# Token rows stored before their norm and scaled after the fetch, token numbers worked out first, and empty rows left out of the fetch

## The chip, the cores and the metric

The kernel runs on one core of a Trainium2 chip. The metric is the device time of one execution in microseconds (us); lower is better. Engines are named as in the profile: PE (matrix), DVE (vector), ACT (scalar), POOL (GpSimd) and SP, which here only issues transfers. Sixteen DMA engines of the core carry the transfers out.

## What is computed

Two decoder layers over 512 tokens of width 1024. Each has a mixer, a cross-attention into 256 memory tokens and a mixture of 32 experts; after each of the three a residual sum is normalised. Only the last part matters here:

```python
def layer_norm(x, g, b, eps=LN_EPS):
    return _standardize(x, eps) * g + b
...
    g_prob = jax.nn.softmax(g_logits, axis=-1)
    grp = jnp.argmax(g_logits, axis=-1)
    ...
    top_v, top_i = lax.top_k(e_logits, MOE_TOPK)
    gate = (jax.nn.softmax(top_v, axis=-1) * p_grp).astype(x.dtype)
    expert = (grp[:, None] * MOE_PER_GROUP + top_i).astype(jnp.int32)
...
        h = jax.nn.silu(xb @ w_gate[e]) * (xb @ w_up[e])
        return h @ w_down[e]
...
        h = layer_norm(DN_ALPHA * h + xa, ln2_g[layer], ln2_b[layer])
        ff = hier_moe(h, ...)
        h = layer_norm(DN_ALPHA * h + ff, ln3_g[layer], ln3_b[layer])
```

A token goes to one of four groups of experts and to two of the eight experts there, so a layer has 1024 pairs of token and expert. An expert has a hidden width of 512; its three weight matrices are 2 MB each in float32.

## The kernel before

**Tiles.** The 512 tokens are four row tiles of 128 (`NT` is 4, `P` is 128). `h` holds them all in SBUF. An expert has 64 slots for tokens, and two experts share the 128 partitions: the lower 64 are one expert's slots, the upper 64 the other's. So there are 16 pairs, objects `X[0]` to `X[15]` of `ExpertRows` (L1660). Slots are filled from number 0 upwards; tokens that find no slot would go through `overflow` (L1757), whose loop runs no time on this input.

**Ahead of the experts.** The output projection of the cross-attention makes row tile after row tile of `h`; after each, `Router.step(i)` (L635) runs: it transposes the tile before (`turn`, PE and two `L612` copies on ACT), works out its router logits, normalises it in place (`norm`, L614, which shares the 1024 columns between DVE, ACT and POOL) and stores it to a DRAM array `rows` by ACT's queue (`store`, L618 and L619). Row 0 of `rows` is zero; token t is row t+1. The logits come from the un-normed transpose, and mean and scale are put in afterwards (L628, L629). `finish` (L647) does the last row tile; its norm lies on ACT (L172) and POOL (L173, L174). The mean and scale of a tile come from a chain of tiny DVE instructions (`ln_3...`, L132 to L160; the figure is the row tile).

**Routing** (L1543 to L1657) is mostly small DVE work: maxima, first-hit masks, ranks, and from these for each token and expert a slot. Then for each of the two choices a one-hot of the slot (L1643, 128x512, tile `hhs`) is multiplied on PE (L1649) with the token's number and gate, which gives a table by slot and pair: `ptab`. Its numbers become `idx` (L1655), its gates `tab`. Both choices' one-hots use one tile.

**A pair.** `gather` (L1680) fetches 128 rows of `rows` by an indirect transfer of POOL's queue into `xg`; an empty slot has number 0 and fetches the zero row. `turn` (L1686) transposes it on PE (`px`, L1693) and DVE copies it to `xT` (two copies, 128x512). `first` multiplies with the gate and up weights (`pg`, `pu`, L1704), L1708 to L1719 make silu(g)*u and transpose it, `second` (L1721) multiplies with the down weights (`py`, L1730) and scales by the gate into `wy` (ACT L1736, then DVE L1737). `combine` (L1740s) adds a pair's rows to `h` by a one-hot product (`pc`) one pair later. `moe` (L1844) writes PE's order of these out by hand; the other engines' is the scheduler's. The fetch for pair n+2 is issued after the transposes of pair n+1, since `xg` is one buffer; pair 15's is issued late, behind `overflow`, and its product closes the layer. `accumulate` (L631, L633) scales `h` for the residual sum once the rows are stored.

**Weights.** A ring of 20 tiles of 1 MB is loaded by SP's queue (L104) in the order of use, 12 loads a pair, each as soon as its tile is free. It fills while routing still runs, and goes on when the first `pg` has read its weights.

## Time and profile before

| | us |
|---|---|
| three timed runs | 1999.49, 1994.82, 1999.64 |
| their median | 1999.49 |
| the profiled execution | 1995.74 |
| its span on the core | 1994.0 |
| PE busy / DVE / ACT / POOL | 1794.0 / 958.7 / 448.9 / 273.9 |
| first pairs apart (layer 0) | 27.45 |
| later pairs apart | 31.09 |

The experts of layer 0 take the span from about 570 to 1030 us, those of layer 1 from about 1497 to 1950. In the rows below a time line has its start, its length, the engine, the line of the code, the operation, what it writes and reads, the shapes, and in brackets how long the engine was idle before and what ended that.

### The profile page before, as it was taken

What the parts mean: (1) busy time and instruction counts of PE and PEld (TensorE: products, weight loads), DVE (VectorE), ACT (ScalarE), POOL (GpSimd) and SP (SyncE); (2) the same over time, 40 slices, a digit from 0 to 9 for tenths busy, and PEclk for the clock granted to TensorE, in tenths of its full rate; (3) what the DMA queues carried; (4) which work ended last, traced back from release to release, by engine and by line L of the source; (5) the groups of instructions that cost most, each with busy time, mean ns of one, the idle gap of its engine ahead of it and who ended that gap; (6) DMA issues with size and microseconds to landing.
All of it is one profiled execution on the core that took longest, in us unless ns stands there. A gap on an engine that the chain in (4) does not pass through costs nothing. (4 is left out here: it accounts for less than half of the span.)

```text
span 1994.0 us, 23447 instructions
## 1 busy us (share of the span) xinstructions
PE 1794.0 (90%) x9206; PEld 1106.6 (55%) x9206; DVE 958.7 (48%) x2053; ACT 448.9 (23%) x834; POOL 273.9 (14%) x226
## 2 busy tenths in 40 slices
PE   8778998999969999989896999989969999989885
PEld 5567876878824334434346866778853334434332
DVE  5686456855633333323326566484572233323325
ACT  6313322343210000000022555443320000000000
POOL 3532433310110000000022100130020000000002
PEclk9887989999979999999998999999979999999998
DMA  5210105464779999999995200243678999999993
GB/s 186 64 63 26 50 1 201 157 201 146 298 302 419 420 420 420 421 421 420 422 373 171 85 22 22 88 143 124 264 283 357 420 420 421 420 420 420 421 420 126
DMA packets 124338, 522.41 MB, mean 262 GB/s; under 512 B 11936, under 2 KB 45888, under 8 KB 75584
## 3 DMA queue, kind: packets, MB, share of 16 engines
q1 hardware_dynamic: 114576, 486.58, 61.7%
q0 software_dynamic: 7056, 25.89, 3.7%
q10 hardware_dynamic: 2592, 8.40, 1.0%
q8 instruction: 74, 1.21, 0.2%
q14 instruction: 40, 0.33, 0.0%
HBM read 506.14 MB, written 14.69 MB: 261 GB/s over the span
## 5 line engine op out<-in xcount | busy, mean ns | idle before, releaser
L1704 PE MATMUL pu<-wu,xT 128*64 128x512 f32 x1024 | 241.9, 595 | 27.7 <-DMA wu<-in_moe_w_up_dram 27.7
L1704 PE MATMUL pg<-wg,xT 128*64 128x512 f32 x1024 | 235.3, 599 | 1.1 <-issue 0.8
L1710 DVE TENSOR_TENSOR hh<-hh,pu 128x512 f32<-128x512 f32 x32 | 22.0, 687 | 444.7 <-PE pu L1704 444.7
L1730 PE MATMUL py<-wd,hh 128*64 128x512 f32 x1024 | 228.9, 596 | 1.6 <-DVE hh L1719 1.6
L1736 ACT ACTIVATE wy<-py,tab 128x512 fp32r<-128x512 f32 x64 | 43.7, 687 | 635.6 <-PE py L1730 635.6
L1704 PEld LDWEIGHTS pu<-wu,xT 128*64 128x64 f32 x1024 | 78.3, 137 | 182.4 <-issue 127.0
L1744 PE MATMUL pc<-wy,wc 128*128 128x512 f32 x480 | 139.2, 420 | 27.8 <-DVE h L1754 27.8
L1704 PEld LDWEIGHTS pg<-wg,xT 128*64 128x64 f32 x1024 | 81.6, 138 | 145.1 <-issue 132.5
L1754 DVE TENSOR_TENSOR h<-h,pc 128x512 f32<-128x512 f32 x240 | 151.0, 680 | 8.6 <-PE pc L1744 8.6
L1683 POOL DMA_INDIRECT xg<-rows,idx x32 | 30.2, 945 | 859.3 <-PE px L1693 716.3
L1730 PEld LDWEIGHTS py<-wd,hh 128*64 128x64 f32 x1024 | 71.1, 137 | 135.5 <-issue 128.8
L1744 PEld LDWEIGHTS pc<-wy,wc 128*128 128x128 f32 x480 | 81.5, 189 | 86.1 <-DVE h L1754 50.4
L1737 DVE SCALAR_TENSOR_TENSOR wy<-py,tab,wy 128x512 fp32r<-128x512 f32 x64 | 47.8, 750 | 169.3 <-ACT wy L1736 165.7
L219 DVE TENSOR_TENSOR wl<-wt,wh 128x1024 fp32r<-128x1024 f32 x37 | 48.0, 1304 | 58.3 <-ACT wh L218 57.9
L218 ACT CAST wh<-wt 128x1024 fp32r<-128x1024 f32 x50 | 51.7, 1049 | 107.5 <-PE ptm L214 61.8
L212 PE MATMUL ptm<-wh,oh 128*128 128x512 f32 x192 | 75.7, 394 | 0.0
L214 PE MATMUL ptm<-wh,ol 128*128 128x512 f32 x192 | 75.0, 391 | 0.0
L213 PE MATMUL ptm<-wl,oh 128*128 128x512 f32 x192 | 75.0, 391 | 0.0
L1708 ACT ACTIVATE hh<-pg 128x512 f32<-128x512 f32 x32 | 19.1, 597 | 229.5 <-PE pg L1704 229.5
L212 PE MATMUL pcm<-xh,wh 128*128 128x512 f32 x144 | 61.9, 430 | 7.1 <-ACT xh L218 6.9
L214 PE MATMUL pcm<-xh,wl 128*128 128x512 f32 x144 | 60.9, 423 | 0.5 <-DVE wl L219 0.5
L213 PE MATMUL pcm<-xl,wh 128*128 128x512 f32 x144 | 60.6, 421 | 0.1
(532 smaller groups left out, 3358.1 us busy)
## 6 DMA issues: line engine op xcount, KB each, us to landing
wg<-in_moe_w_gate_dram SPq DMA_DIRECT2D x128, 1024.0 KB, 19.8
wu<-in_moe_w_up_dram SPq DMA_DIRECT2D x128, 1024.0 KB, 21.1
wd<-in_moe_w_down_dram SPq DMA_DIRECT2D x124, 1024.0 KB, 20.1
wr<-in_ab_w_in_dram SPq DMA_DIRECT2D x8, 1024.0 KB, 7.8
wr<-in_xa_wkv_dram SPq DMA_DIRECT2D x8, 1024.0 KB, 11.4
wt<-in_xa_wkv_dram SPq DMA_DIRECT2D x8, 1024.0 KB, 5.2
wr<-in_xa_wq_dram SPq DMA_DIRECT2D x8, 1024.0 KB, 6.3
wt<-in_xa_wo_dram SPq DMA_DIRECT2D x8, 1024.0 KB, 7.3
```

The lines of the kernel that those rows point to most:

```text
L212: nc.tensor.matmul(out, lh, rh, start=start, stop=False)
L213: nc.tensor.matmul(out, lh, rl, start=False, stop=False)
L214: nc.tensor.matmul(out, ll, rh, start=False, stop=stop)
L218: k.nc.scalar.copy(hi, src)
L219: (eng or k.low()).tensor_tensor(lo, src, hi.bitcast(F32), op=ALU.subtract)
L1683: nc.gpsimd.indirect_dma_start(out=self.xg, out_offset=None, in_=k.rows[:, :], in_offset=IndirectOffsetOnAxis(ap=self.idx(), axis=0))
L1704: nc.tensor.matmul(ps[j * M:(j + 1) * M, :], self.xT[:, half * 4 + kk, j * M:(j + 1) * M], w[j][:, kk, :], start=(half == 0 and kk == 0), ...
L1730: nc.tensor.matmul(py[n][j * M:(j + 1) * M, :], self.hT[:, half * 2 + kk, j * M:(j + 1) * M], w[j][:, kk, n * 512:(n + 1) * 512], start=(h ...
L1736: nc.scalar.activation(yh, py[n], AF.Copy, scale=self.tab()[:, 1:2])
L1737: nc.vector.scalar_tensor_tensor(yl, py[n], self.tab()[:, 1:2], yh.bitcast(F32), op0=ALU.mult, op1=ALU.subtract)
L1744: self.k.nc.tensor.matmul(ps, self.C[:, i * P:(i + 1) * P], y, start=start and not last, stop=last)
L1754: k.nc.vector.tensor_add(k.h[:, i, s], k.h[:, i, s], pc)
```

## The change

- `rows` has 1026 columns. `store(i)` runs at the start of `step(i)`, so the row tile is stored before its norm. Two further columns hold its scale r and -mean*r: POOL copies them to a tile `rn`, and ACT's queue stores it. The zero row is now the last, number T, and token t is row t.
- The first three row tiles are still normalised in `step`, the last one by four DVE instructions (`last_norm`) written behind the fetches.
- `routing` works out the token numbers first: both one-hots (two tiles now) times `num`, a table of 16 columns, give `pidx` and from it `idx`. The fetch of `X[0]` follows, and only then the gates and `tab`.
- A fetch checks its row numbers against a bound. Those above it, the empty slots, aren't fetched and the slot keeps what it had; the first pair, the last and the overflow have the bound one higher and fetch the zero row.
- After the fetch `scale` multiplies by r and adds -mean*r in place (ACT, 128x1024) and POOL puts 1 and 0 into the two columns. ln2's gain and bias are put in where the transposed tile leaves PSUM: four instructions on DVE and four on ACT (128x128 each) in place of two DVE copies. They come from a tile `ch`, two small loads per layer.
- Pair n+1's `scale` stands in the code ahead of pair n's `first("g")`.

```diff
+
+ROW = D + 2
...
-    def norm(self, i, share=256):
-        k = self.k
-        k.layer_norm(k.h[:, i, :], *self.ln[i], share=share)
+    def norm(self, i):
+        self.k.layer_norm(self.k.h[:, i, :], *self.ln[i])
+
+    def last_norm(self):
+        V, n = self.k.nc.vector, NT - 1
+        (m, r, nm), g, b = self.ln[n]
+        for j in range(2):
+            t, s = self.k.h[:, n, j * 512:(j + 1) * 512], slice(j * 512, (j + 1) * 512)
+            V.scalar_tensor_tensor(t, t, m, g[:, s], op0=ALU.subtract, op1=ALU.mult)
+            V.scalar_tensor_tensor(t, t, r, b[:, s], op0=ALU.mult, op1=ALU.add)
 
     def store(self, i):
-        self.k.nc.scalar.dma_start(self.k.rows[1 + i * P:1 + (i + 1) * P], self.k.h[:, i])
+        self.k.nc.scalar.dma_start(self.k.rows[i * P:(i + 1) * P, :D], self.k.h[:, i])
...
     def step(self, i, scale, g, b):
 
         self.ln[i] = (scale, g, b)
+        self.store(i)
+        for j in range(2):
+            self.k.nc.gpsimd.tensor_copy(self.rn[:, i, j:j + 1], scale[1 + j])
+        self.k.nc.scalar.dma_start(self.k.rows[i * P:(i + 1) * P, D:D + 2], self.rn[:, i])
...
         self.norm(i - 1)
-        self.store(i - 1)
...
-        self.norm(n, D)
-        self.store(n)
...
+    rowoh = [hot([NT, P]), pool.tile([P, NT, P], F32R, name="rowoh1")]
+    ptb = k.psum("y", name="pidx")
+    pohs = []
+    for j in range(2):
+        poh = tl([NT, 16], f"poh{j}")
+        pohs.append(poh)
+        V.tensor_reduce(poh, o32[j].rearrange("p i (a b) -> p i a b", b=2), axis=AX.X, op=ALU.add)
...
+        V.scalar_tensor_tensor(row, row, -2.0 * SPAN, key[:, j], op0=ALU.mult, op1=ALU.add)
+        V.tensor_tensor(rowoh[j], c["code"][:, None, :].to_broadcast([P, NT, P]),
+                        row[:, :, None].to_broadcast([P, NT, P]), op=ALU.is_equal)
+        num = pool.tile([P, NT, 16], F32R, name=f"num{j}")
+        V.tensor_tensor(num, poh, c["tokno"][:, :, None].to_broadcast([P, NT, 16]), op=ALU.mult)
+        for i in range(NT):
+            nc.tensor.matmul(ptb[:, :16], rowoh[j][:, i, :], num[:, i], start=(j == 0 and i == 0),
+                             stop=(j == 1 and i == NT - 1))
+    idx = keep.tile([P, 16], I32, name="idx")
+    V.tensor_scalar(idx, ptb[:, :16], float(T), None, op0=ALU.add)
+    rt.update(idx=idx)
+    yield
...
-    tab = tl([16, 2], "tab")
-    pt2 = ptb[:, :32].rearrange("p (a b) -> p a b", b=2)
-    idx = tl([16], "idx", I32)
-    V.tensor_copy(idx, pt2[:, :, 0])
-    V.tensor_copy(tab, pt2)
...
-    def gather(self):
+    def gather(self, empty=False):
         k, nc = self.k, self.k.nc
-        self.xg = self.pool.tile([P, D], F32, name="xg", tag="xg", bufs=1)
+        self.xg = self.pool.tile([P, ROW], F32, name="xg", tag="xg", bufs=1)
+
         nc.gpsimd.indirect_dma_start(out=self.xg, out_offset=None, in_=k.rows[:, :],
-                                     in_offset=IndirectOffsetOnAxis(ap=self.idx(), axis=0))
+                                     in_offset=IndirectOffsetOnAxis(ap=self.idx(), axis=0),
+                                     bounds_check=T if empty else T - 1, oob_is_err=False)
+
+    def scale(self):
+        x = self.xg
+        self.k.nc.scalar.activation(x[:, :D], x[:, :D], AF.Identity, scale=x[:, D:D + 1], bias=x[:, D + 1:D + 2])
+
+        self.k.nc.gpsimd.tensor_copy(x[:, D:], self.k.cst["oneno"])
...
         k, nc = self.k, self.k.nc
+        g, b = (k.router.ch[:, j] for j in range(2))
         self.xT = self.work("xT", n=D).rearrange("p (i n) -> p i n", n=P)
         for q in range(2):
             pt = k.psum("t", name="px")
             for j in range(4):
                 kk = q * 4 + j
-                nc.tensor.transpose(pt[:, j * P:(j + 1) * P], self.xg[:, kk::KD], k.cst["ident"])
-            nc.vector.tensor_copy(self.xT[:, q * 4:q * 4 + 4, :], pt.rearrange("p (a b) -> p a b", a=4))
+                nc.tensor.transpose(pt[:, j * P:(j + 1) * P], self.xg[:, kk:D:KD], k.cst["ident"])
+            for j in range(4):
+                kk = q * 4 + j
+                gk, bk, pk = g[:, kk:kk + 1], b[:, kk:kk + 1], pt[:, j * P:(j + 1) * P]
+                if q == 0:
+                    nc.vector.tensor_scalar(self.xT[:, kk, :], pk, gk, bk, op0=ALU.mult, op1=ALU.add)
+                else:
+                    nc.scalar.activation(self.xT[:, kk, :], pk, AF.Identity, scale=gk, bias=bk)
...
-            routing(k, k.pool(s1, f"rtt{l}"), rp, work, rt, l)
-            X[0].gather()
+            route = routing(k, k.pool(s1, f"rtt{l}"), rp, work, rt, l)
+            next(route)
+            X[0].gather(True)
+            run(route)
+            X[0].scale()
+            X[0].turn()
+            X[1].gather()
+            k.router.last_norm()
             for i in range(NT):
                 k.router.accumulate(i)
-            X[0].turn()
-            X[1].gather()
         with tc.manual_schedule(engines={mybir.EngineType.PE}):
             for n, x in enumerate(X):
                 more = n + 1 < len(X)
+                if more and n + 1 != len(X) - 1:
+                    X[n + 1].scale()
                 x.first("g")
                 x.first("u")
...
@@ -1881,8 +1933,8 @@
                     X[n - 1].combine(2, "cccc")
                     W.load_until_spare()
                     overflow(k, pool, work, l, rt)
-                    X[n + 1].gather()
-                    x.turn_hidden(), x.second(), x.scatter(), X[n + 1].turn()
+                    X[n + 1].gather(True)
+                    x.turn_hidden(), x.second(), x.scatter(), X[n + 1].scale(), X[n + 1].turn()
                     continue
                 x.turn_hidden()
```

**DVE, end of the mean-and-scale chain of row tile 3, up to routing's first instruction.** Before (`ln_3y` is the scale worked out in steps, `L<-plog` and `L<-sg` the logits, L1560 the start of routing):

```order
L146 SCALAR_TENSOR_TENSOR ln_3y<-ln_3t,ln_3y 128x1
L629 SCALAR_TENSOR_TENSOR L<-sg,ln_2nm,L 128x36
L140 SCALAR_TENSOR_TENSOR ln_3t<-ln_3y,ln_3x 128x1
L146 SCALAR_TENSOR_TENSOR ln_3y<-ln_3t,ln_3y 128x1
L140 SCALAR_TENSOR_TENSOR ln_3t<-ln_3y,ln_3x 128x1
L146 SCALAR_TENSOR_TENSOR ln_3y<-ln_3t,ln_3y 128x1
L160 SCALAR_TENSOR_TENSOR ln_3nm<-ln_3mv,ln_3y 128x1
L628 SCALAR_TENSOR_TENSOR L<-plog,ln_3y,sb 128x36
L629 SCALAR_TENSOR_TENSOR L<-sg,ln_3nm,L 128x36
L1560 TENSOR_REDUCE xTs<-L 128x4
```

After (L633 and L634 are `last_norm`, L646 and L647 the logits; the next instruction is L1580, the start of routing):

```order
L633 SCALAR_TENSOR_TENSOR h<-h,ln_3mv,lng 128x512
L140 SCALAR_TENSOR_TENSOR ln_3t<-ln_3y,ln_3x 128x1
L647 SCALAR_TENSOR_TENSOR L<-sg,ln_2nm,L 128x36
L146 SCALAR_TENSOR_TENSOR ln_3y<-ln_3t,ln_3y 128x1
L633 SCALAR_TENSOR_TENSOR h<-h,ln_3mv,lng 128x512
L140 SCALAR_TENSOR_TENSOR ln_3t<-ln_3y,ln_3x 128x1
L146 SCALAR_TENSOR_TENSOR ln_3y<-ln_3t,ln_3y 128x1
L160 SCALAR_TENSOR_TENSOR ln_3nm<-ln_3mv,ln_3y 128x1
L646 SCALAR_TENSOR_TENSOR L<-plog,ln_3y,sb 128x36
L634 SCALAR_TENSOR_TENSOR h<-h,ln_3y,lnb 128x512
L647 SCALAR_TENSOR_TENSOR L<-sg,ln_3nm,L 128x36
L634 SCALAR_TENSOR_TENSOR h<-h,ln_3y,lnb 128x512
```

The four instructions that norm row tile 3 now stand among the chain's steps, ahead of routing, though they are written behind the fetches.

**ACT, the store of row tile 3.** Before:

```order
L612 COPY hT_4310<-ptr 128x512 x2
L172 ACTIVATE h<-h,ln_2nm,ln_2y 128x256
L633 ACTIVATE h<-h 128x1024
L612 COPY hT_4342<-ptr 128x512 x2
L619 DMA rows_3951<-h 128x1024
L172 ACTIVATE h<-h,ln_3nm,ln_3y 128x1024
L633 ACTIVATE h<-h 128x1024
L619 DMA rows_3951<-h 128x1024
L1616 ACTIVATE xTs<-xTs 128x16
```

After (`rn` is the tile of the two extra columns; L637 is `store`, L651 `accumulate`):

```order
L659 DMA rows_3953<-rn 128x2
L623 COPY hT_4328<-ptr 128x512
L637 DMA rows_3953<-h 128x1024
L623 COPY hT_4328<-ptr 128x512
L172 ACTIVATE h<-h,ln_2nm,ln_2y 128x256
L623 COPY hT_4359<-ptr 128x512 x2
L651 ACTIVATE h<-h 128x1024
L659 DMA rows_3953<-rn 128x2
```

The store stands one place behind the first `ptr` copy of row tile 2, two copies and an `accumulate` ahead of where it stood, and ACT's share of the last norm (L172 with `ln_3nm`) is gone.

**DVE, from the first one-hot to `idx`.** Before:

```order
L1643 TENSOR_TENSOR hhs<-cst,xTs 128x512
L1642 SCALAR_TENSOR_TENSOR xTs<-xTs,key 128x4
L1646 TENSOR_TENSOR rhs_4516<-xTs,val_4492 128x128
L1769 TENSOR_SCALAR onb<-R 128x32
L1781 TENSOR_SCALAR ot<-R 128x128
L1771 SCALAR_TENSOR_TENSOR onb<-R,onb 128x32
L1782 SCALAR_TENSOR_TENSOR ot<-R,ot 128x128
L1643 TENSOR_TENSOR hhs<-cst,xTs 128x512
L1771 SCALAR_TENSOR_TENSOR onb<-R,onb 128x32 x2
L1773 SCALAR_TENSOR_TENSOR oinc<-cst,onb 128x32
L1655 CAST idx<-ptab 128x16
```

After (L1646 are the one-hots, L1813 to L1825 belong to `overflow`, L1673 to L1679 to the gates):

```order
L1646 TENSOR_TENSOR hhs<-cst,xTs 128x512
L1645 SCALAR_TENSOR_TENSOR xTs<-xTs,key 128x4
L1673 RECIPROCAL val_4534<-val_4534 128x4
L1813 TENSOR_SCALAR onb<-R 128x32
L1646 TENSOR_TENSOR rowoh_4498<-cst,xTs 128x512
L1674 TENSOR_TENSOR val_4534<-val_4534,xTs 128x4
L1815 SCALAR_TENSOR_TENSOR onb<-R,onb 128x32
L1825 TENSOR_SCALAR ot<-R 128x128
L1675 TENSOR_TENSOR val_4535<-val_4534,xTs 128x4
L1679 TENSOR_TENSOR xTs<-xTs,val_4534 128x128
L1654 TENSOR_SCALAR idx<-pidx 128x16
```

The second one-hot stands three places behind the first and has its own tile; `idx` comes from `pidx`, which holds no gates.

## Rows read from the trace of the kernel before

**Rows 1.** Page, busy time by engine (section 1) and the queue of POOL (section 3).

```profile
PE 1794.0 (90%) x9206; PEld 1106.6 (55%) x9206; DVE 958.7 (48%) x2053; ACT 448.9 (23%) x834; POOL 273.9 (14%) x226
...
q0 software_dynamic: 7056, 25.89, 3.7%
```

**Rows 2.** Windows of the expert stretches: busy us by engine, granted clock, DMA share, GB/s.

```profile
core 0: us, PE busy (x) PEld busy (x) DVE busy (x) ACT busy (x) POOL busy (x), PEclk, DMA share, GB/s
577.00:805.00 228.00, 219.27 (x1028) 90.70 (x1024) 72.99 (x138) 16.26 (x25) 7.50 (x8) 1.00 1.01 417
...
1735.00:1950.00 215.00, 191.98 (x863) 82.88 (x863) 64.94 (x123) 13.80 (x21) 5.62 (x6) 1.00 1.01 420
```

**Rows 3.** Timeline of PE in layer 0's experts: start, length, engine, line, instruction.

```profile
625.06 7.04 PE L1704 MATMUL pg<-wg,xT 128*64 128x512 f32 x32
...
652.51 7.04 PE L1704 MATMUL pg<-wg,xT 128*64 128x512 f32 x32
...
912.31 7.20 PE L1704 MATMUL pg<-wg,xT 128*64 128x512 f32 x31
...
943.40 7.21 PE L1704 MATMUL pg<-wg,xT 128*64 128x512 f32 x31
...
987.38 3.65 PE L1704 MATMUL pu<-wu,xT 128*64 128x512 f32 x14 [1.32 <-DMA wu<-in_moe_w_up_dram]
```

**Rows 4.** Timeline of DVE, end of the rsqrt chain to the token numbers, layer 0.

```profile
546.04 0.15 DVE L146 SCALAR_TENSOR_TENSOR ln_3y<-ln_3t,ln_3y 128x1 f32<-128x1 f32 x1
...
548.21 0.17 DVE L1560 TENSOR_REDUCE xTs<-L 128x4 f32<-128x16 f32 x1
...
548.84 2.25 DVE L1575 TENSOR_SCALAR xgs<-xgs 128x16 f32<-128x16 f32 x1
...
551.78 1.99 DVE L1569 TENSOR_TENSOR xgs<-xgs,xTs 128x128 f32<-128x128 f32 x1
...
554.99 0.17 DVE L1618 TENSOR_REDUCE xTs<-xTs 128x4 f32<-128x16 f32 x1 [0.76 <-ACT xTs L1616]
...
556.06 0.28 DVE L1569 TENSOR_TENSOR xgs<-xgs,xTs 128x128 f32<-128x128 f32 x1
...
559.29 0.68 DVE L1643 TENSOR_TENSOR hhs<-cst,xTs 128x512 f32<-128x512 f32 x1
...
561.99 0.69 DVE L1643 TENSOR_TENSOR hhs<-cst,xTs 128x512 f32<-128x512 f32 x1 [1.19 <-PE ptab L1649]
...
564.69 0.17 DVE L1655 CAST idx<-ptab 128x16 int32<-128x16 f32 x1 [1.42 <-PE ptab L1649]
```

**Rows 5.** Timeline of POOL, its share of the norm of row tile 3.

```profile
548.73 2.34 POOL L173 TENSOR_TENSOR h<-h,lng 128x1024 f32<-128x1024 f32 x1 [4.20 <-ACT h L172]
551.15 2.47 POOL L174 TENSOR_TENSOR h<-h,lnb 128x1024 f32<-128x1024 f32 x1
```

**Rows 6.** Timeline of PE, the slot tables.

```profile
560.03 1.92 PE L1649 MATMUL ptab<-rhs,hhs 128*128 128x32 f32 x8 [2.25 <-DVE hhs L1643]
562.73 1.92 PE L1649 MATMUL ptab<-rhs,hhs 128*128 128x32 f32 x8 [0.78 <-DVE hhs L1643]
```

**Rows 7.** DMA issues: transfer, queue, count, (KB each,) median us from issue to landing.

```profile
rows<-h ACTq DMA_DIRECT2D x8, 512.0 KB, 7.6
...
xg<-rows,idx POOLq DMA_INDIRECT x32, 9.1
```

**Rows 8.** Timeline of ACT around the stores of row tiles 2 and 3.

```profile
541.13 1.07 ACT L612 COPY hT<-ptr 128x512 f32<-128x512 f32 x2 [5.69 <-PE ptr L611]
...
545.90 0.33 ACTq L619 DMA_DIRECT2D rows<-h  x1
547.41 1.24 ACT L172 ACTIVATE h<-h,ln_3nm,ln_3y 128x1024 f32<-128x1024 f32 x1 [2.60 <-DVE ln_3nm L160]
553.79 1.06 ACT L633 ACTIVATE h<-h 128x1024 f32<-128x1024 f32 x1 [5.14 <-DMA rows<-h]
```

**Rows 9.** Chain of waits, the last pair of layer 1: start, length, what.

```profile
1922.64 9.07 DMA xg<-rows,idx
```

More of the change, by code (lines that the diff above doesn't have):

```diff
@@ L561, in __init__ @@
         self.L = p.tile([P, NT, 36], F32, name="L")
+        self.rn = p.tile([P, NT, 2], F32, name="rn")
+        self.ch = p.tile([P, 2, KD], F32, name="ch")
         self.hT = {0: self.copy(0)}
         v = self.copy(1).rearrange("p a b -> p (a b)")
[L566 to L567 removed]
+        k.rows = k.dram.tile([1 + T, ROW], F32, name=f"rows{l}")
+        zero = tmp.tile([114, ROW // 114], F32, name="zero")
         nc.vector.memset(zero, 0.0)
[L569 removed]
+        nc.scalar.dma_start(k.rows[T:T + 1].rearrange("o (p k) -> (o p) k", p=114), zero)
         self.wr, self.w2 = (v[:, o:o + KD * n].rearrange("p (k n) -> p k n", k=KD) for o, n in ((0, 36), (KD * 36, 72)))
@@ L1474, in get, with scratch @@
         return self.views[name]
-    def scratch(self, name, n):
-        t, used = self.pool.tile([P, n], F32, name=name + "s", tag=name, bufs=1), [0]
+    def scratch(self, name, n, dt=F32):
+        t, used = self.pool.tile([P, n], dt, name=name + "s", tag=name, bufs=1), [0]
         def make(shape, dt=F32):
@@ L1546, in routing @@
     h = k.h
-    kept = ("tab", "idx", "key", "R", "o32", "val0", "val1")
+    kept = ("key", "R", "o32")
     first = ("ge", "gr", "sel", "x0e", "x0r", "x1e", "x1r", "ohb", "tm")
-    early, late, hot = work.early, work.late, work.scratch("hh", FF)
+    early, late, hot = work.early, work.late, work.scratch("hh", FF, F32R)
     def tl(shape, name, dt=F32):
-        if name in kept or name in ("rhs0", "rhs1"):
-            return (keep if name in kept else pool).tile([P] + list(shape), dt, name=name)
+        if name in kept:
+            return keep.tile([P] + list(shape), dt, name=name)
         return (early if name in first else late)(shape, dt)
@@ L1622, in routing @@
     nc.scalar.activation(ex, ex, AF.Exp)
-    vals = [tl([NT, 2], f"val{j}") for j in range(2)]
+    vals = [keep.tile([P, NT, 2], F32, name=f"val{j}") for j in range(2)]
     for j in range(2):
@@ L1630, in routing @@
     V.tensor_tensor(gt[1], gt[0], ex, op=ALU.mult)
[L1631 removed]
     ptb = k.psum("y", name="ptab")
[L1633 removed]
     for j in range(2):
[L1635 to L1646 removed]
+        rhs = late([NT, 32]).rearrange("p i (a b) -> p i a b", b=2)
+        V.tensor_tensor(rhs, pohs[j][:, :, :, None].to_broadcast([P, NT, 16, 2]),
                         vals[j][:, :, None, :].to_broadcast([P, NT, 16, 2]), op=ALU.mult)
         for i in range(NT):
[L1649 to L1657 removed]
+            nc.tensor.matmul(ptb[:, :32], rowoh[j][:, i, :].bitcast(F32), rhs[:, i].rearrange("p a b -> p (a b)"),
+                             start=(j == 0 and i == 0), stop=(j == 1 and i == NT - 1))
+    tab = keep.tile([P, 16, 2], F32, name="tab")
+    V.tensor_copy(tab, ptb[:, :32].rearrange("p (a b) -> p a b", b=2))
+    rt.update(key=key, o32=o32, tab=tab, vals=vals)
 class ExpertRows:
@@ L1839, in overflow @@
             x.hidden = lambda: x.xg[:, :FF]
-            x.scatter(), x.gather(), x.turn(), x.first("g"), x.first("u"), x.turn_hidden(), x.second(), x.combine()
+            x.scatter(), x.gather(True), x.scale(), x.turn(), x.first("g"), x.first("u"), x.turn_hidden(), x.second(), x.combine()
             V.tensor_scalar(cur, cur, 1.0, None, op0=ALU.add)
@@ L1907, in moe @@
         g = k.bcast(pool, A["ln3_g"][l], D, "g3", t=work.get("xT"))
-        b = k.bcast(pool, A["ln3_b"][l], D, "b3", tag="xg")
+        b = k.bcast(pool, A["ln3_b"][l], D, "b3", t=pool.tile([P, ROW], F32, name="b3", tag="xg", bufs=1)[:, :D])
         if filler:
@@ L1979, in constants @@
     add("tokid", p[:, None] + P * np.arange(NT)[None, :] + 1)
+    add("tokno", p[:, None] + P * np.arange(NT)[None, :] - T)
+    add("oneno", np.tile([1.0, 0.0], (P, 1)))
     add("krow", KD * p[:, None] + np.arange(KD)[None, :])
```

32 lines of the change are left out of this document (10 added, 22 removed).

## The prediction

> **What bounds the kernel now.** I read the page's busy shares first: PE is busy 90% of the span, which by itself says PE-bound [rows 1]. The stretch table says otherwise for the expert stretches of both layers (one window of each stands in the rows). There PE's clock is granted in full, the busy share of the DMA engines is 1.01, and 417 to 420 GB/s flow [rows 2]. PE's timeline then shows two regimes. Early pairs start 27.45 us apart (625.06 to 652.51), which is PE's own work on weights that were loaded ahead. Later pairs start 31.09 us apart (912.31 to 943.40), because `pu` waits for `wu` [rows 3]. A pair moves 12 MB of weights and 0.52 MB of gathered rows, 13.1 MB; at 420 GB/s this is 31.2 us, the later spacing. So from the first pair on the weight stream never rests, and a layer ends at: the moment that the first `pg` starts to free ring tiles and so restarts the stream, plus all bytes at 420 GB/s up to the last `wu` (waited for at 987.38), plus a fixed tail that begins with the last pair's gather. Three terms follow: what moves the first `pg`, what takes bytes out of the stream, what lengthens the tail.
>
> **Term 1, the way to the first `pg`, per layer.** In the kernel before, routing's first instruction on DVE runs at 548.21 and `idx` is written at 564.69 to 564.86, 16.65 us [rows 4]. Two DVE instructions stand out: L1575 takes 2.25 us and L1569 1.99 us. POOL's two steps of the norm of row tile 3 run at 548.73 to 551.07 and 551.15 to 553.62 [rows 5], and the two DVE instructions end within 0.15 us of them. The same L1569 on the same shape takes 0.28 us at 556.06, with POOL idle. After the change POOL has no norm to do there. I take 1.7 us off the one and 2.05 us off the other (down to about 0.2, as its small neighbours), 3.75 together. The wait for ACT's exponential (0.76 us, L1618) and some 0.4 us of gate instructions move behind `idx`: 1.15. The second one-hot waited 1.19 us for PE to have read the first, since both shared one tile, and `idx` waited another 1.42 for the second group of matmuls. With two tiles the two one-hots (0.68 each, from 559.29) follow each other with small work between, so the second ends near 560.9 in place of 562.68. A group of matmuls took 1.92 us of PE, from 560.03 and again from 562.73 [rows 6]: at that length the second group now starts at 561.95 and `idx` is 0.8 us earlier; with 16 columns in place of 32 and a shorter type, groups of half the length would make it 2.7. I take 2.4. Together −7.3 us from routing's start to `idx`.
>
> Against this stands the new order. The four DVE instructions that norm row tile 3 are placed by the scheduler between the rsqrt steps, ahead of routing. The first overwrites `h` and so waits until that tile's store has read it. The store is issued behind the first `ptr` copy on ACT, near 541.7 (the two copies take 1.07 from 541.13). A store takes 7.6 us in the median; the trace's store of 545.90 released ACT at 553.79, 7.9 later [rows 7, 8]. So DVE stands from about 546.2 to 549.4, and queued behind it are the rest of the rsqrt chain, the last logits and all of routing; PE, POOL's gather and the first `pg` wait for that in turn. After the store about 4.2 us remain to run (four of 0.74 and eight small ones of some 0.2, partly overlapping). Routing starts near 553.6 in place of 548.21, +5.4. `idx` is then 1.9 us earlier. The fetched tile must also be scaled on ACT before it is transposed: 1.06 to 1.24 us for an in-place 128x1024 there [rows 8], and some 0.3 for the extra hop. First `pg`: −1.9 + 1.45 = **−0.45 us per layer**, between −3 and +2. Row tiles 0 to 2 have a wait of the same kind before their norms, by the same reckoning under 2 us and on rows whose norm PE doesn't need; I cost it at nothing, and if the cover of PE's matmuls fails it is 1.5 us. The little stores of mean and scale come on ACT's queue near 553, 10 us before the gather needs them: nothing, and 1 us for each us beyond these 10. Zeroing and storing the last row, and two small `ch` loads on SP, lie in the prelude before it: nothing.
>
> **Term 2, the bytes.** Of 2048 slots 1024 hold a token (512 tokens, two experts each), so a gather of 128 rows loses 64 on average. Pairs 2 to 14 gather inside the busy stretch: 13 x 64 x 4096 B = 3.4 MB, 8.1 us at 420 GB/s per layer, 16.2 for both if the sixteen engines shed it evenly. The other bound is nothing: a transfer is finished when its slowest engine is, slots are filled from 0 upwards, so the empty ones are the high slots of each expert's 64 and may not be spread evenly; or a left-out row still costs its turn. From outside, the packets of the POOL queue cost 3.7% of 16 engines' span for 7056, 167 ns each [rows 1]; with 104 gathered packets per engine and layer in the stretch, the whole is 17.4 us, and the saving is what part of these the fullest engine loses. Share 1.01 in the busy stretch says that all engines are full at once now, so an engine that loses less will lag. I take the middle, half of each: **−8.1 us for both layers**, with 0 and −16.2 as ends.
>
> On which engine a row lies no row here shows. The Trainium skill, page "DMA: Bandwidth & Descriptors", section "The descriptor swizzle", states that in a 128-partition transfer engine 0 writes partitions 0 to 3 and 32 to 35, engine 1 the next four of each, and so on, with engines 8 to 15 on the upper 64. By that rule the engine with the first slots keeps the most rows; for this routing it would lose 33 of its 104 packets in layer 0 and 21 in layer 1, an estimate of 9.0 us in all at the measured packet price, where an even spread would give twice as much; the trace can't confirm it.
>
> **Cost of longer rows.** Rows are 4104 B in place of 4096 and no longer aligned. By bytes this is 0.2%, nothing; if the odd end costs half a packet more on the 832 kept rows (52 per engine, 167 ns), 4.3 us per layer. No row shows it; the 8 added bytes are nearest to the first end, so I take 0.5 per layer, **+1.0**.
>
> **Inside the stream.** ACT's order becomes silu, four `xT` evictions, the next pair's scale, then the two `wy`. The scale waits for a fetch issued after the transposes. With 9.1 us from issue to landing [rows 7] it holds `wy` back some 4 us. `wy` is read by `pc`, after the next pair's `pg` and `pu`, 14 us on, and DVE's share of 0.3 leaves it room [rows 2]. So nothing; if a fetch took 20 us, each us more would cost one us per pair. The eight evictions hide beside `py` (32 matmuls like `pg`'s, 7 us of PE [rows 3]).
>
> **Term 3, the tail, per layer.** The chain of waits shows the last gather on the path: `xg`, 9.07 us from 1922.64 [rows 9], and the transposes `px` wait for it. Pair 15 fetches its empty slots too, so the fetch is as long as before. The scale comes in between, 1.06 to 1.24 and a hop, and no work hides it: **+1.15**, +2.3 for both.
>
> **Sum**, on the profiled execution's 1995.74: −0.9 (term 1, two layers) − 8.1 + 1.0 + 2.3 = −5.7, 1990.0. The profiled execution lies between the three timed runs (1994.82, 1999.49, 1999.64). The same 5.7 below their median is 1993.8; I name the point between, 1992.
>
> **Rivals.** *Even relief*: every engine sheds half its rows; −0.9 − 16.2 + 1.0 + 2.3 = −13.8, 1981.9. For it: share 1.01 on average, and gathers of several pairs could balance each other. Against it: all fill from slot 0. *No relief* (the bound doesn't do what it says: a left-out row still takes its turn on its engine, or the fullest engine keeps all of its rows): −0.9 + 0 + 1.0 + 2.3 = +2.4, 1998.1. For it: the fetch has as many entries in `idx` as before. *Late store*, slower: place, DVE at the first of the four norm instructions, both layers. If row tile 3's store lands 14 us after issue and not 7.8, routing starts 6.2 us later and the sum is −5.7 + 12.4 = +6.7, 2002.4. It decides from there with half the relief, and from 1.8 us of lateness per layer with none. For it: `wu` loads fill the queues then. Against it: the stores before had those beside them too, and took 7.6.
>
> **How the numbers follow.** Chances: half the relief 0.45, even relief 0.24, no relief 0.20, late store 0.11. A measurement of this kernel tells about 0.3%, 6 us, from no change. Half the relief, at −5.7, falls just about on that line: 0.24 faster, 0.21 same. Even relief is faster. No relief is same. So faster 0.48, same 0.41, slower 0.11. Range: from even relief, 1981, to no relief measured against the median (1999.49 + 2.4 is 2001.9), cut to 2001; left out are the late store, what of even relief lies lower, and what of no relief lies higher, under 2 in 10.
>
> **What would show it.** In the profile after: DVE idle some 3 us at the first 128x512 norm instruction, released by the `rows` store (right), or 8 and more (late store); L1575's and L1569's counterparts near 0.2 and 0.3 us; `idx` about 2 us earlier; the distance of the first `pg` from the last `wu` wait of pair 14 shorter by 4 us per layer (half), 8 (even), 0 (none); a scale of about 1.1 us in the last chain. What would make it wrong: a stream that is no longer set by bytes, or `pg` waiting for a scale in each pair.

## The result, and the profile after

The changed kernel takes 1985.84 us (median of five runs, 1983.48 to 1989.51) against 1999.49 before, a ratio of 0.9938 with a 95% interval of 0.9924 to 0.9952: 12 to 14 us faster. The profiled execution takes 1984.65 against 1995.74. The range held the time, and the direction is that of the forecast; by the prediction's own line of 6 us it is faster, which had a chance of 0.48. The size is not the forecast one: on the profiled execution 5.7 us were forecast and 11.1 came.

The time splits at the places that the prediction named. First the kernel before, then the one after, in PE's timeline: the first `pg` of a layer, the last wait of a `pu` for `wu` (pair 14), and the `pg` of pair 15 (lines left out between them; the wait at 987.38 is in [rows 3]; a `pg` with fewer than 32 instructions is cut off by the end of the stretch that was asked for).

```profile
571.66 8.73 PE L1704 MATMUL pg<-wg,xT 128*64 128x512 f32 x32
...
1008.72 3.65 PE L1704 MATMUL pg<-wg,xT 128*64 128x512 f32 x16 [0.38 <-issue]
...
1497.55 8.29 PE L1704 MATMUL pg<-wg,xT 128*64 128x512 f32 x32
...
1912.28 3.65 PE L1704 MATMUL pu<-wu,xT 128*64 128x512 f32 x14 [1.32 <-DMA wu<-in_moe_w_up_dram]
...
1933.36 7.09 PE L1704 MATMUL pg<-wg,xT 128*64 128x512 f32 x32 [0.38 <-issue]
```

```profile
572.59 7.68 PE L1748 MATMUL pg<-wg,xT 128*64 128x512 f32 x32
...
977.49 3.65 PE L1748 MATMUL pu<-wu,xT 128*64 128x512 f32 x14 [1.03 <-DMA wu<-in_moe_w_up_dram]
...
1000.63 2.83 PE L1748 MATMUL pg<-wg,xT 128*64 128x512 f32 x6 [0.52 <-DVE xT L1736]
...
1491.54 8.99 PE L1748 MATMUL pg<-wg,xT 128*64 128x512 f32 x32
...
1898.87 3.65 PE L1748 MATMUL pu<-wu,xT 128*64 128x512 f32 x14 [1.01 <-DMA wu<-in_moe_w_up_dram]
...
1921.86 7.21 PE L1748 MATMUL pg<-wg,xT 128*64 128x512 f32 x32 [0.51 <-DVE xT L1736]
```

I call the way from the first `pg` to that wait the stream, and from there to the `pg` of pair 15 the tail; the prelude of layer 1 runs from the one layer's last such `pg` to the next one's first.

| us | before | after | difference |
|---|---|---|---|
| first `pg`, layer 0 | 571.66 | 572.59 | +0.9 |
| stream, layer 0 | 415.72 | 404.90 | −10.8 |
| tail, layer 0 | 21.34 | 23.14 | +1.8 |
| prelude, layer 1 | 488.83 | 490.91 | +2.1 |
| stream, layer 1 | 414.73 | 407.33 | −7.4 |
| tail, layer 1 | 21.08 | 22.99 | +1.9 |

Together −11.5; the spans differ by 11.4 (1994.0 and 1982.6). So preludes and tails lost more than forecast (6.7 for −0.9 + 2.3), and the streams gained more than the upper bound that I had set for them (18.2 against 16.2). The windows say why the rows left out can't explain it alone. The same two stretches, before and then after (columns as in [rows 2]):

```profile
640.00:950.00 310.00, 288.56 (x1327) 123.19 (x1327) 105.16 (x197) 21.09 (x32) 10.31 (x11) 1.00 1.01 420
1570.00:1880.00 310.00, 288.69 (x1325) 122.84 (x1325) 100.45 (x189) 21.68 (x33) 10.30 (x11) 1.00 1.01 421
```

```profile
640.00:950.00 310.00, 292.55 (x1355) 122.59 (x1355) 104.49 (x218) 49.39 (x88) 13.13 (x22) 1.00 1.01 425
1570.00:1880.00 310.00, 291.49 (x1346) 123.06 (x1344) 104.31 (x214) 48.10 (x85) 12.12 (x21) 1.00 1.01 426
```

There are fewer bytes, and the bytes that are left flow faster: 425 GB/s in place of 420, at the same DMA share. 1.2% of 415 us is 4.9 us per layer, half of what the streams gained.

The page's row for POOL's queue (the counterpart in [rows 1]) shows the rows left out:

```profile
q0 software_dynamic: 7056, 18.68, 2.8%
```

The packets are as many as before and the bytes 7.21 MB fewer. The trace's record of single packets shows why: 1766 packets of 4 B stand where rows were (by the routing of this input, 896 and 870 slots of pairs 1 to 14 are empty in the two layers). In the two stretches such a packet took 9 ns and a fetched row 161 ns (162 before). The packets of the queue took 1170 us of engine time before and 903 after (the 3.7% and 2.8%), so 151 ns were saved for each row left out. A row that is left out still counts as a packet but takes next to no time.

The prelude, on DVE and in the order of time (after, layer 0):

```profile
550.39 0.75 DVE L633 SCALAR_TENSOR_TENSOR h<-h,ln_3mv,lng 128x512 f32<-128x512 f32 x1 [5.23 <-DMA rows<-h]
...
554.26 0.16 DVE L1580 TENSOR_REDUCE xTs<-L 128x4 f32<-128x16 f32 x1
...
554.89 0.17 DVE L1595 TENSOR_SCALAR xgs<-xgs 128x16 f32<-128x16 f32 x1
...
555.74 0.29 DVE L1589 TENSOR_TENSOR xgs<-xgs,xTs 128x128 f32<-128x128 f32 x1
...
560.60 0.68 DVE L1646 TENSOR_TENSOR hhs<-cst,xTs 128x512 fp32r<-128x512 f32 x1
...
561.41 0.69 DVE L1646 TENSOR_TENSOR rowoh<-cst,xTs 128x512 fp32r<-128x512 f32 x1
...
563.24 0.17 DVE L1654 TENSOR_SCALAR idx<-pidx 128x16 int32<-128x16 f32 x1 [0.56 <-PE pidx L1651]
```

DVE waits 5.23 us for the store, and routing begins at 554.26, 6.05 later than before. The counterparts of L1575 and L1569 take 0.17 and 0.29 us, and `idx` is there 8.98 us after routing's start, 7.5 sooner than before ([rows 4]: 16.48). The store itself and the scale that follows the fetch, on ACT, and between them the fetch's issue on POOL:

```profile
540.33 0.33 ACTq L637 DMA_DIRECT2D rows<-h  x1
...
563.70 1.18 POOL L1713 DMA_INDIRECT xg<-rows,idx  x1 [10.77 <-DMA wd<-in_moe_w_down_dram]
...
569.40 1.24 ACT L1719 ACTIVATE xg<-xg 128x1024 f32<-128x1024 f32 x1 [10.36 <-DMA xg<-rows,idx]
```

The store was issued at 540.33 and let DVE go at 550.39: 10.1 us, not 7.8. The fetch took 5.70 us from its issue to the scale. In the kernel before it took 4.63 to the transposes:

```profile
565.14 1.03 POOL L1683 DMA_INDIRECT xg<-rows,idx  x1 [11.52 <-DMA wd<-in_moe_w_down_dram]
...
569.77 1.97 PE L1693 MATMUL px<-cst,xg 128*128 128x128 f32 x8 [5.12 <-DMA xg<-rows,idx]
```

### The profile page after: what moved, and what is told of

It is laid out like the page before. It is cut to its first block, busy times and chain, and to the rows that moved or that the text cites. A ratio compares the mean times of both kernels' runs of the same rounds, so it can differ in the third digit from the quotient of the medians.

```text
span 1982.6 us, 23918 instructions
## 1 busy us (share of the span) xinstructions
PE 1794.6 (91%) x9222; PEld 1104.2 (56%) x9222; DVE 953.8 (48%) x2129; ACT 529.6 (27%) x992; POOL 274.8 (14%) x270
## 3 DMA queue, kind: packets, MB, share of 16 engines
q0 software_dynamic: 7056, 18.68, 2.8%
## 5 line engine op out<-in xcount | busy, mean ns | idle before, releaser
L1748 PE MATMUL pu<-wu,xT 128*64 128x512 f32 x1024 | 237.1, 594 | 14.6 <-DMA wu<-in_moe_w_up_dram 14.6
L1748 PEld LDWEIGHTS pg<-wg,xT 128*64 128x64 f32 x1024 | 76.1, 139 | 150.7 <-issue 132.8
L1738 ACT ACTIVATE xT<-px,ch 128x128 f32<-128x128 f32 x128 | 48.1, 456 | 380.9 <-PE px L1731 380.7
L1719 ACT ACTIVATE xg<-xg 128x1024 f32<-128x1024 f32 x32 | 39.7, 1240 | 279.7 <-DMA xg<-rows,idx 279.7
```

Source lines behind the costliest of these rows:

```text
L1719: self.k.nc.scalar.activation(x[:, :D], x[:, :D], AF.Identity, scale=x[:, D:D + 1], bias=x[:, D + 1:D + 2])
L1738: nc.scalar.activation(self.xT[:, kk, :], pk, AF.Identity, scale=gk, bias=bk)
L1748: nc.tensor.matmul(ps[j * M:(j + 1) * M, :], self.xT[:, half * 4 + kk, j * M:(j + 1) * M], w[j][:, kk, :], start=(half == 0 and kk == 0), ...
```

## The experiments

Ten kernels, each with the same three numbers per layer, read as above. The first column is the first `pg` of layer 0, the fourth the prelude of layer 1. Kernels with the same code ahead of the first `pg` differ there by some 4 us from execution to execution (569.5 to 573.9 for those with the old prelude), so only the streams and single waits are compared from one execution. A time is a median against the kernel before, run in turn with it. The kernel before came out at 1999.49 beside the changed kernel, at 1998.53 beside the first four of the table and at 1997.59 beside the others, so a distance from the changed kernel is uncertain by some 2 us. GB/s are those of the window from 640 to 950.

| kernel | first `pg` | stream 0 | tail 0 | prelude 1 | stream 1 | tail 1 | GB/s | ratio to before (interval) |
|---|---|---|---|---|---|---|---|---|
| all slots fetched | 573.92 | 410.51 | 23.46 | 489.58 | 411.21 | 23.13 | 426 | 0.9979 (0.9969 to 0.9989) |
| slots dealt out | 574.78 | 404.92 | 23.23 | 488.95 | 404.11 | 23.28 | 425 | 0.9912 (0.9897 to 0.9928) |
| late norm | 566.02 | 411.23 | 24.08 | 482.63 | 412.32 | 23.35 | 420 | 0.9907 (0.9890 to 0.9925) |
| leave-out alone | 570.69 | 410.81 | 21.41 | 491.27 | 410.48 | 21.34 | 420 | 0.9951 (0.9933 to 0.9968) |
| before, 128 B moved | 570.38 | 411.35 | 21.68 | 490.17 | 410.35 | 21.04 | 425 | 0.9951 (0.9938 to 0.9965) |
| after, 32 B moved | 574.37 | 411.26 | 24.05 | 491.72 | 411.11 | 23.40 | 420 | 0.9989 (0.9980 to 0.9998) |
| all together | 567.36 | 404.05 | 23.33 | 484.17 | 404.59 | 23.30 | 425 | 0.9855 (0.9840 to 0.9870) |
| before, 64 B moved | 571.21 | 417.26 | 21.39 | 489.06 | 415.74 | 21.55 | 420 | one run, 1998.64 us |
| before, the other eight moved | 569.47 | 414.64 | 22.62 | 487.17 | 411.40 | 22.70 | 424 | one run, 1990.40 us |
| before, both moved | 573.87 | 412.92 | 22.60 | 487.63 | 409.87 | 21.22 | 426 | one run, 1992.19 us |

**All slots fetched.** The change without the leave-out:

```diff
-                                     bounds_check=T if empty else T - 1, oob_is_err=False)
+                                     bounds_check=T, oob_is_err=False)
```

> The changed kernel with the bound raised by one in every fetch, so that all empty slots fetch the zero row again; nothing else differs, and all of the result is computed. The profiled executions of before and after differ by 11.1 us, made up of a weight stream shorter by 18.2 us (both layers, from the first pg to the last wait for wu), preludes longer by 3.0 and tails longer by 3.7. Theory A: the whole 18.2 comes from the rows left out. Then this kernel is some 18 us slower than the changed one, 7 slower than the one before, and the expert stretches go back to 420 GB/s. Theory B: only about 9 of it comes from the rows; the other half is weight transfers that run faster (425 in place of 420 GB/s) for another reason in the change. Then it is about 9 us slower than the changed one and the stretches keep 424 or more.

Its median is 1994.83 us, 9.0 above the changed kernel, still under the kernel before, and its stretch kept the rate:

```profile
640.00:950.00 310.00, 289.72 (x1334) 122.79 (x1334) 106.02 (x220) 49.47 (x88) 13.31 (x22) 1.00 1.01 426
```

This is theory B: the rows are worth 9.5 us of stream in all (821.72 less 812.23), and something else in the change made the transfers faster.

**Leave-out alone**, on the kernel before. The zero row comes last, the numbers count from 0, rows stay normed and 4096 B long (the lines that matter):

```diff
-    V.tensor_copy(idx, pt2[:, :, 0])
+    V.tensor_scalar(idx, pt2[:, :, 0], float(T), None, op0=ALU.add)
...
-                                     in_offset=IndirectOffsetOnAxis(ap=self.idx(), axis=0))
+                                     in_offset=IndirectOffsetOnAxis(ap=self.idx(), axis=0),
+                                     bounds_check=T if empty else T - 1, oob_is_err=False)
```

> The kernel before with the leave-out alone: zero row last, token numbers counted from 0, the bound in the fetches of pairs 1 to 14; rows still stored normed with 1024 columns, routing in its old order, no scale after the fetch. All of the result is computed. If the leave-out carries the gain by itself: the stretch is 18 us shorter in all, prelude and tail as before, so some 18 us faster than the kernel before, and faster than the changed one by 6 to 7. If half of the 18.2 came from the other parts of the change: 9 us faster than before, and 420 to 421 GB/s in the stretches.

1988.99 us against 1998.53 for the kernel before in the same comparison. The streams are 9.2 us shorter in sum (821.29 against 830.45), at the old rate:

```profile
640.00:950.00 310.00, 291.06 (x1343) 121.43 (x1341) 104.26 (x196) 21.70 (x33) 10.91 (x11) 1.00 1.01 420
```

So by both ways, undone in the one kernel and done alone in the other, leaving the rows out is worth 9 to 9.5 us, a little over half of the evenly shared 16.2. With the code of tails and preludes untouched, this small part alone gives most of what the whole change gives (0.9951 against 0.9938; the intervals overlap).

**Slots dealt out.** Is it the fullest engine that keeps the other half?

```diff
-    add("code", np.tile(p // CAP * SPAN + p % CAP, (P, 1)))
+    add("code", np.tile(p // CAP * SPAN + ((p % CAP // 32) * 4 + p % 4) * 8 + p // 4 % 8, (P, 1)))
```

> The changed kernel with one constant permuted: the slots of an expert are dealt out over its 64 partitions so that groups of four partitions fill in turn, and not from partition 0 upwards. Same number of rows left out, all of the result is computed. Theory of the fullest engine (partitions 0 to 3 and 32 to 35 hang on one DMA engine and so on, and the stretch ends with the fullest): the engine with the most rows now loses about 51 of 104 packets per layer in place of 33 and 21; 49 more packets at 160 ns, some 7 to 8 us faster than the changed kernel. Theory of even relief (the engines share the rows evenly already): no change, within 2 us.

1981.94 us, 3.9 below the changed kernel (all six executions lie below all five of that kernel, though the intervals of the two ratios overlap). The gain is there, though not 7 to 8. I had taken an even share of 51 packets lost on each engine, but a pair's two experts don't hold the same number of tokens: counted out from the routing (by the prediction's rule of which engine writes which partitions), the engine with the most rows loses 46 and 41 of 104 packets (layers 0 and 1) where the changed kernel's loses 33 and 21, which is 33 packets more, 5.0 us at 151 ns. In the streams layer 1 shows its 3.2 us (407.33 to 404.11; 20 packets are 3.0), layer 0 nothing of its 2.0 in this execution. The last kernel of this section is dealt out too and has its weights in the same place; its streams are 2.7 (layer 1) and 0.9 (layer 0) shorter. The end of layer 1's weights points the same way. Windows after the last pair's weights are issued, before and then after:

```profile
1944.00:1948.00 4.00, 4.00 (x19) 1.70 (x16) 0.57 (x1) 0.00 (x0) 0.00 (x0) 1.00 0.99 407
1948.00:1952.00 4.00, 4.00 (x19) 2.85 (x18) 4.00 (x8) 0.00 (x0) 0.00 (x0) 1.00 1.03 410
1952.00:1956.00 4.00, 4.00 (x12) 1.44 (x10) 2.46 (x7) 0.00 (x0) 0.00 (x0) 1.00 0.59 235
1956.00:1960.00 4.00, 4.00 (x20) 1.27 (x20) 0.00 (x0) 0.00 (x0) 0.00 (x0) 1.00 0.00 0
```

```profile
1930.00:1934.00 4.00, 4.00 (x20) 1.29 (x18) 0.00 (x0) 0.00 (x0) 0.00 (x0) 1.00 0.91 375
1934.00:1938.00 4.00, 4.00 (x20) 2.24 (x17) 1.95 (x4) 0.00 (x0) 0.00 (x0) 1.00 0.56 216
1938.00:1942.00 4.00, 4.00 (x16) 2.18 (x15) 3.52 (x7) 0.00 (x0) 0.00 (x0) 1.00 0.58 196
1942.00:1946.00 4.00, 4.00 (x14) 1.34 (x14) 1.56 (x5) 0.00 (x0) 0.00 (x0) 1.00 0.00 0
```

Before, the sixteen engines run full and stop within one window. After, the share falls to 0.91, 0.56 and 0.58 over 12 us, which fits engines that have done their part while others still work. The shape alone proves little: with the slots dealt out the windows read 1.00, 0.81, 0.78 and 0.01 (from 1927), but with the leave-out alone, whose rows lie as unevenly as the changed kernel's, 0.87, 0.91 and 0.19 (from 1936). In the middle of the stretch nothing is seen (1.01 in all); that an engine which is ahead goes on with the next tile's packets there, so that only the last tile's end counts, is an inference.

**Late norm**: the wait for the store on DVE. The order has its cause in the memory plan: `last_norm` reads gain, bias, mean and scale from the cross-attention's tiles, and routing's scratch takes their space. So the four values were first put elsewhere (gain and bias copied by ACT into two tiles that are free by then), and the norm queued behind `idx`:

```diff
+        self.last_gb = [self.copy(n + 1 + j).rearrange("p a b -> p (a b)") for j in range(2)]
+        for t, s in zip(self.last_gb, self.ln[n][1:]):
+            self.k.nc.scalar.copy(t, s)
...
-            k.router.last_norm()
+            with tc.issue_after(rt["last"].ins):
+                k.router.last_norm()
```

> The changed kernel with the norm of row tile 3 queued on DVE behind the token numbers: gain and bias are first copied by ACT into two tiles that are free by then (2 x 1.05 us), mean and scale by POOL, so that the norm no longer holds the memory that routing's scratch needs. All of the result is computed. If the wait for the store on DVE (5.2 us per layer, with routing behind it) is what the prelude lost, routing starts some 5 us earlier, the first pg too, and the whole is about 10 us faster than the changed kernel. If the token numbers then wait for something else, the stored rows or their scale above all (the store lands near 550, that of scale and mean some 7 us after its issue), less than 4 us.

1981.18 us, 4.7 below the changed kernel and not 10. The prelude did what was expected: first `pg` 6.6 us earlier in layer 0 and 8.3 in layer 1. But the streams are 11.3 us longer in sum (823.55 against 812.23), for the rate is 420 again:

```profile
640.00:950.00 310.00, 290.60 (x1335) 119.95 (x1336) 99.62 (x210) 49.40 (x88) 13.13 (x22) 1.00 1.01 420
```

A new tile of 8 bytes and a norm elsewhere can hardly slow weight transfers down, other than by where things lie. So I compared where the tiles lie, by the kernels' memory plans, in the kernels with 425 GB/s and in those with 420. Ten of the twenty weight tiles (8192 B per partition each, packed behind the router's tiles) start at a multiple of 512 B in SBUF in the changed kernel, 384 past one in the kernel before (tables that are 32 B longer, `rn` with 32 B and `ch` with 64 B make the 128 B of difference), and 32 past one in the late norm, whose new tile takes 32 B. Of the others eight lie 320 past one before and 352 after; the last two (480 and 448) take one load each per layer, so that eighteen tiles carry the stream.

**Before, 128 B moved.** Nothing but an unused tile:

```diff
+        p.tile([P, 32], F32, name="pad")
         self.hT = {0: self.copy(0)}
```

> The kernel before with one unused tile of 128 bytes per partition put ahead of the tiles of the router, and nothing else. It moves ten of the twenty weight tiles (of 8192 bytes per partition) from byte 384 past a multiple of 512 in SBUF to a multiple of 512, which is where the changed kernel happens to have them; the other ten don't move. So far the three kernels with these ten at a multiple of 512 (the changed one, all slots fetched, slots dealt out) moved 425 GB/s in the expert stretches, the three with another place (before, leave-out alone: 384 past; late norm: 32 past) 420. Theory of the place: 425 GB/s, both streams some 4.5 us shorter, about 9 us faster than the kernel before. Theory that the faster stream comes from the order or the longer rows: 420 GB/s and no change.

1987.99 us against 1997.59: 9.6 us for a tile that nobody uses. (Besides the ten weight tiles it moves only the router's two transposed tiles, which lie ahead of them.)

```profile
640.00:950.00 310.00, 290.05 (x1337) 122.67 (x1338) 103.82 (x195) 21.69 (x33) 10.33 (x11) 1.00 1.01 425
```

The record of single packets shows the rate from below: in the two stretches an 8192 B packet of weights takes 314.1 to 314.5 ns on average in the five kernels with 420 GB/s and 309.9 to 310.9 in the seven others. In this kernel nine in ten of them take 309 to 313 ns (309 to 320 in the kernel before), though eight of the eighteen tiles have not moved. So packets into those became faster too.

**After, 32 B moved.** The other direction, the same line with `[P, 8]` in the changed kernel:

> The changed kernel with an unused tile of 32 bytes per partition ahead of the transposed tiles of the router, and nothing else, so that the ten weight tiles start 32 bytes past a multiple of 512 as in the late-norm kernel. Theory of the place: 420 GB/s, about 9 us slower than the changed kernel, which leaves 3 to 4 us gained on the kernel before. If the place has nothing to do with it: 425 GB/s and no change.

1995.80 us, 10.0 above the changed kernel, and the gain on the kernel before is down to 0.1% (0.9989, up to 0.9998).

```profile
640.00:950.00 310.00, 291.56 (x1344) 123.06 (x1339) 105.97 (x220) 49.40 (x88) 13.13 (x22) 1.00 1.01 420
```

This is what the change as it was meant is worth without the luck of its place: 8.1 us off the streams, nearly all of it spent again in preludes and tails (in the profiled execution, one of the slower of its eleven, 10.6).

**Three more places.** 64 B in the kernel before puts the ten at 448 past a multiple of 512:

> The kernel before with an unused tile of 64 bytes: the ten weight tiles at 448 past a multiple of 512 (a multiple of 64, not of 128). If what counts is a multiple of 256 or 512: 420 GB/s as at 384. If it is something finer about these tiles and the others: a rate between or another one.

420 GB/s and streams as before. Then the other tiles, which had stayed put so far. The expectations speak of ten; they are the eight that lie 320 past one:

> The kernel before with 192 unused bytes per partition behind h, so that the weight tiles of the first three rings (ten of twenty) start at a multiple of 512 bytes and the other ten 64 past one. So far only the place of the other ten was moved. If every tile pays for its own place: a rate halfway, as the kernel with the other ten in place would be one too, but that one moved 425 GB/s with nearly all packets short, so I expect 420 GB/s, and streams near 415 us per layer. If the place of either ten is enough: 425 GB/s and streams near 411.

> The kernel before with 64 unused bytes behind h and 64 ahead of the router's transposed tiles: the ten tiles ringed last stay at a multiple of 512, the first ten lie 384 past one in place of 320. If the place of the last ten alone decides: 425 GB/s, streams near 411 us per layer, as with 128 bytes at one place. If the distance between the two groups of tiles decides: another rate.

With the eight at a multiple of 512 and the ten 64 past one the rate is 424; with the ten in place and the eight moved to 384 past one it is 426. My first expectation of the two was wrong: either group in place is enough for nearly the whole rate (the two windows below, in this order). Each is one execution, and the first shows only 4.4 us less stream, where 128 B gave 8.8.

```profile
640.00:950.00 310.00, 288.24 (x1324) 120.39 (x1324) 103.54 (x194) 21.69 (x33) 10.30 (x11) 1.00 1.01 424
...
640.00:950.00 310.00, 289.52 (x1333) 123.58 (x1331) 106.12 (x198) 21.08 (x32) 10.30 (x11) 1.00 1.01 426
```

Their three tails of 22.6 and 22.7 have another cause: there `py` of pair 14 took 9.4 to 9.7 us in place of 7.1. In the first kernel's layer 0 it ran in part at the lower of TensorE's two levels (1.2 GHz; granted clock 0.50 from 996 to 1000), after PE had waited for DVE.

**All together.** The late norm without the new tile (the mean is worked out from the two numbers in `rn`), so that the place stays, and the slots dealt out:

```diff
+        r, nm = (self.rn[:, n, j:j + 1] for j in range(2))
+        m = pool.tile([P, 1], F32, name="m3")
+        V.reciprocal(m, r)
+        V.scalar_tensor_tensor(m, m, -1.0, nm, op0=ALU.mult, op1=ALU.mult)
```

> The changed kernel with the late norm of row tile 3 (this time its mean is worked out again from the two stored numbers, so that no tile is added and the ten weight tiles stay at a multiple of 512) and the slots dealt out over the partitions. If the three effects add (place kept, norm behind the token numbers 7 to 8 us per layer as first measured in the stretch ahead of pg, slots some 3 us): 425 GB/s, first pg near 566 and 17 to 19 us faster than the changed kernel, near 1968. If the first pg is now held by another wait or the even slots give nothing: 10 to 14 us faster.

1969.19 us, 16.6 below the changed kernel (17 to 19 were expected) and 1.45% below the one before (0.9855, 0.9840 to 0.9870): it beats both. The first `pg` comes 5.2 us sooner in layer 0 and the prelude of layer 1 is 6.7 shorter, the streams 3.6 in sum, the tails 0.5 longer; 15.0 in sum, and the spans differ by 15.1. DVE no longer stands at the norm:

```profile
556.06 0.17 DVE L1661 TENSOR_SCALAR idx<-pidx 128x16 int32<-128x16 f32 x1 [0.56 <-PE pidx L1658]
...
559.62 1.41 DVE L637 SCALAR_TENSOR_TENSOR h<-h,m,hT 128x512 f32<-128x512 f32 x2
```

`idx` is 7.2 us earlier than in the changed kernel, the first `pg` 5.2: the fetch, issued at 556.51, now takes until 564.17, 7.7 us and not 5.7; why is open.

## Why the prediction was right and wrong, step by step

- **What bounds the kernel: right.** The stream sets the expert stretches. Time taken off the streams, by fewer bytes or a faster flow of the rest, comes out of the span one to one, as the sums above show.
- **Term 2, the rows left out: right, with some luck in the size.** 8.1 forecast; 9.2 done alone, 9.5 when undone. The 8.1 was the middle of two bounds and not worked out from the rows of each engine. The mechanism between the bounds is, as far as the runs go, the named one: the engine with the most rows sets the end. It rests on the kernels with the slots dealt out, which got 3.2 and 3.6 us more off the streams with the same rows left out.
- The Trainium skill's rule (page "DMA: Bandwidth & Descriptors", section "The descriptor swizzle": engine 0 writes partitions 0 to 3 and 32 to 35, and so on) gave an estimate of 9.0 us for the leave-out (8.2 at the 151 ns measured for a row) and, counted again, 5.0 more with the slots dealt out. The runs agree with the first (9.2 and 9.5) and show a part of the second (3.2 and 3.6 of stream). No row names an engine, so the rule itself is borne out by these sizes only.
- **What failed: the rate.** The stream was reckoned at 420 GB/s, as if the change could not touch it. It moved ten weight tiles by 128 B in SBUF, and the rate rose to 425: 8.8 us off the streams in the kernel before with 128 unused bytes, 9.6 us in time. Without it the changed kernel stands at 1995.80, and the forecast of −5.7 would have been 3 to 4 us too good (its ratio, 0.9989, is 2.2 us). So the rate is more than the whole of the difference in size: it gave some 10 us that were not forecast, and preludes and tails took back 3 to 5 that were not forecast either. That the time came out about 6 us from the named 1992 is in part luck, since the two misses have opposite signs. No row of before could have shown the rate; the diff could at least have raised the question, since each added tile moves what lies behind it.
- **Term 1, the prelude: mechanism right, three sizes off.** The gain inside routing came as worked out (7.5 for 7.3). The wait for the store was seen, but the store took 10.1 us from issue and not 7.8, issued 1.4 earlier than I put it; DVE stood 5.23 us for some 3, and routing started 6.05 later, for 5.4. The larger miss is the step from `idx` to `pg`: I charged 1.45 for the scale; the scale took 1.24 and its hop 0.05, but the fetch before it also took longer, 5.70 and 6.00 us from issue to the scale against 4.63 and 4.82 to the transposes before. Why is open: with the bound alone it was 4.91 and 5.21, with long rows and no leave-out 5.47 and 5.62 (this first fetch always fetches its empty slots). The two together give about −0.5 forecast and +0.9 and +2.1 measured.
- **Term 3, the tail: right, low.** 1.15 forecast, 1.8 and 1.9 measured: scale and hop 1.3, 0.2 for the evictions in eight pieces, and half a us ahead of the fetch that I did not trace. In layer 1 `py` of pair 14 took 9.3 us in place of 7.1, in part at the lower level of TensorE's clock (granted 0.59 on average from 1912 to 1916) after PE had waited for DVE, but it ended at 1920.04 and the scale at 1920.13, so it did not add to the tail.
- **Longer rows: nothing, not +1.0.** The long-row kernels' streams sum to 822.4 (32 B moved) and 821.7 (all fetched, in place), their counterparts with 4096 B to 821.3 and 821.7: between 0 and 1.1. The record of single packets decides: in the two stretches a row of 4104 B took 162.7 ns in the kernel with 420 GB/s and 160.4 in the one with 426, one of 4096 B 162.0 and 160.0 in their counterparts. With 104 rows per engine and layer this is under 0.1 us, and the other bound, half a packet more, is out.
- **Inside the stream: right.** The scale in ACT's queue and the eight evictions left no wait; 425 GB/s at a share of 1.01 shows the stream full in both windows.
- **The rivals.** By the median alone even relief would look right: −13.8 forecast for it, −13.7 between the medians. It is not: some 9 us from uneven relief, some 9 from the place, and the losses in preludes and tails happen to give the same sum. Late store was partly true (10.1 us for 7.8) and far from the 14 that it needed.

## What to carry to other kernels

Where a stream of equal transfers sets the pace, a gain has three sources that look alike in the total: fewer bytes, fewer bytes on the fullest engine, and a better rate; read the GB/s of the same stretch in both traces before any story is told. When a change adds or resizes a tile, note where the tiles behind it come to lie, and test a difference in time against a kernel in which nothing but an unused tile differs. And a part that is done alone (here the bound) may be worth nearly as much as the whole.

## What the runs showed of the hardware that was not expected

- The place of weight tiles in SBUF changes the rate of their transfers: 424 to 426 GB/s in the seven kernels with ten (in one of them eight) of the eighteen tiles of the stream at a multiple of 512 B, 420 in the five with none there (those had the ten 32, 384 or 448 past one, and the eight 320 or 352). Why, and why one group in place makes the packets into the other faster too, is not explained; whether 256 past a multiple of 512 would do was not run.
- Two DVE instructions of 0.17 and 0.29 us took 2.25 and 1.99 us as long as POOL worked on 128x1024 operands beside them, and ended within 0.15 us of POOL's; without POOL's work they were short. The prediction had read this from the trace before, and the trace after bears it out.
- A row left out by the bound is still a packet in the queue's count (7056 in both kernels), of 4 B and 9 ns in place of 4096 B and 162.
